# A DeltaNet and block-attention layer on one core: opening rebuilt, part of the low halves on GpSimd, order anew

## Chip, core and metric

The kernel runs on one core of one Trainium2 chip. The metric is device time in microseconds (us) of one execution; 236.81 us is the median of three runs of the kernel before (236.16 to 237.06). TensorE does the matrix work, VectorE and ScalarE elementwise work, GpSimd nearly nothing, and SyncE (SP) issues the DMAs.

## What is computed

One decoder layer for 256 tokens of width 1024, all in float32. `h` is a normalised `x`, scaled and shifted per column by two linear functions of a condition `c`. One wide product `h @ w_in` gives the inputs of two branches (gated DeltaNet with a short causal convolution; block attention, which for one block of 256 is causal attention) and the gates. Each branch is projected, the two are mixed, projected again, normalised, gated and added to `x`.

```python
shift, scale, gate = split(silu(c) @ w_ada + b_ada, 3)
h = rms_norm(x, g_pre) * (1 + scale) + shift
qkv_dn, z_dn, beta_logit, a_logit, qkv_mb, z_mb, merge_logit = split(h @ w_in, cuts)
qkv_dn = silu(causal_depthwise_conv(qkv_dn, conv_w))
o_dn = gated_delta_rule_chunked(l2_normalize(q_dn), l2_normalize(k_dn), v_dn, g, beta)
y_dn = (rms_norm(o_dn, dn_norm_g) * silu(z_dn)) @ w_proj_dn
y_mb = (moba_attention(q_mb, k_mb, v_mb) * silu(z_mb)) @ w_proj_mb
mixed = (sigmoid(m_dn) * y_dn + sigmoid(m_mb) * y_mb) @ w_out
out = x + gate * rms_norm(mixed, g_post)
```

## The kernel before

**Who sets the order.** `block_kernel` calls engine methods on a `Machine`, which records each one as an operation with its dependences (L107) and prices it (`price`, L125). `schedule` (L169) then lists all operations by rank, the longest priced way to the end, plus a number per stage from the table `BOOST` (L52); `issue` (L235) emits them. All instructions therefore have line 236 in the trace, and each engine runs its list strictly in order. `TURN` (L51) prices a change of TensorE between full-size matmuls, transposes and small-tile matmuls.

**Precision.** Weights and activations are split: `split` (L327) makes `whi`, a rounded copy, on ScalarE, and `wlo`, the rest (`raw` minus `whi`), on VectorE. Each product is three matmuls: hhi·whi, hlo·whi, hhi·wlo.

**Buffers and loads.** A weight chunk is 128 x 1024 (512 KB). There are 4 buffers `raw`, 5 `whi`, 5 `wlo`, 4 `wss`; all loads are issued by SP, one after the other in a fixed order, and a `raw` buffer is free for the next load only when its `wlo` has been made.

**Opening.** Loads: the small parameters `pr`, the two halves of `x` (128 tokens each), `wss` for k = 0, then `w1` and `wss` by turns (`load_k`, L353). TensorE runs warm-up matmuls and broadcasts silu(c) to all partitions (`scb`, L377, kept in buffer AT). Stage "x" (L388): ScalarE sums the squares of each half of `x`, VectorE makes 1/rms and a diagonal matrix `dg` (buffer pex), and 16 fp32 matmuls `xs @ dg` scale and transpose `x` into four PSUM banks. `ada(k)` (L419) makes shift and scale for 128 columns by two VectorE dot products of `wss` with AT. `h_ops(k)` (L431) makes hhi (ScalarE), a full copy (`cv`) and hlo (VectorE).

**First GEMM** (`phase1`, L438; stages "first", "cut", "mod", "ada"): eight steps k, each with two chunks of `w1`, 16 column blocks of 128, and three matmuls for each: 48 matmuls, into eight PSUM banks.

**After it:** `gemm_v` (L511, i = 6: value columns and the logits `lgw`), convolution, `gemm(i)` (L532, 15 jobs over `w2`, two chunks each, 48 matmuls each), norm (L601: transposes of q and k; ScalarE squares them for the norm, writing `jk`), attention scores (`mk`, `mq`, L642), the DeltaNet chunks, gates, projections, output. `gemm` matmuls are interleaved with all small work.

## Time and profile before

| | |
|---|---|
| median of 3 runs | 236.81 us (236.16 to 237.06) |
| the profiled execution's own time | 236.04 us |
| its span in the trace | 234.3 us |
| TensorE busy | 221.3 us, 1902 instructions |
| VectorE busy | 195.9 us, 442 |
| ScalarE busy | 142.4 us, 281 |
| GpSimd busy | 1.2 us, 7 |
| moved by DMA | 51.20 MB, mean 219 GB/s |

The page counts busy time per engine; the span is what the trace covers, and the execution's own time has 1.7 us more around it. Matmuls overlap in TensorE's pipeline and their ends are modelled, so a busy TensorE is judged by the distance of the starts. The idle time in square brackets stands ahead of an instruction, with what ended it.

### The profile page before, as it was taken

To read this page: it belongs to the slowest core of one execution; us is meant where nothing else is said; L and a number is where in the kernel's file an instruction comes from. 1 tells how busy PE (TensorE), PEld (TensorE's weight loads), DVE (VectorE), ACT (ScalarE), POOL (GpSimd) and SP (SyncE) were. 2 spreads that over 40 slices of the span, in tenths; PEclk is the share of its full clock that TensorE was granted. 3 is DMA by queue.
4 is the path that set the end of the run, shared out by engine and by line. 5 is a ranking of instruction groups with operands and counts; after the bars stand their busy time and mean duration, and the time that the engine had idled before them with its cause. 6 is when DMAs were issued, how large, how long until landed. Compare 5 with 4: busy or idle time off the path is not lost.

```text
span 234.3 us, 4925 instructions
## 1 busy us (share of the span) xinstructions
PE 221.3 (94%) x1902; PEld 209.0 (89%) x1902; DVE 195.9 (84%) x442; ACT 142.4 (61%) x281; POOL 1.2 (1%) x7
## 2 busy tenths in 40 slices
PE   8699999998999999999999999999999989999990
PEld 8699999997999998899789999888789979899980
DVE  0789998889899996499989999897899989668864
ACT  6585665556899589965416556445597943355341
POOL 1000000000000000000000000000000000000000
PEclk9799999999999999999999999999999999999999
DMA  7999999784879765252732507745396980297004
GB/s 220 377 413 406 411 404 388 280 304 158 314 238 312 233 220 183 91 179 65 267 120 92 180 21 236 228 131 174 94 369 246 261 289 26 70 325 236 0 29 153
DMA packets 15271, 51.20 MB, mean 219 GB/s; under 512 B 1680, under 2 KB 2064, under 8 KB 15248
## 3 DMA queue, kind: packets, MB, share of 16 engines
q1 hardware_dynamic: 15248, 50.89, 62.6%
q8 instruction: 15, 0.25, 0.4%
q14 instruction: 8, 0.07, 0.1%
HBM read 49.83 MB, written 1.05 MB: 217 GB/s over the span
## 4 chain that ended last, share of the span: by engine, by line
PE 50%; DMA 20%; DVE 14%; ACT 10%; issue 3%; SPq 1%; DVEq 0%; ACTq 0%
PE bank_g L236 32%; PE bank_d L236 14%; DMA raw<-in_w 10%; DMA wss<-in_wss 5%; PE bank_m L236 5%; DVE wlo L236 4%; ACT whi L236 3%; DVE wss L236 2%; ACT L236 2%; DMA raw<-in_wpj 2%; ACT jk L236 2%; DVE xT L236 2%; DMA raw<-in_wv 2%; DVE vT L236 1%; SPq L236 1%
## 5 line engine op out<-in xcount | busy, mean ns | idle before, releaser
L236 ACT CAST whi<-raw 128x1024 fp32r<-128x1024 f32 (+2 forms) x68 | 67.1, 993 | 38.3 <-DMA raw<-in_w 14.7
L236 DVE TENSOR_TENSOR wlo<-raw,whi 128x1024 fp32r<-128x1024 f32 (+2 forms) x68 | 77.8, 1158 | 8.0 <-ACT whi L236 6.7
L236 PE MATMUL bank_g<-hhi,whi 128*128 128x256 f32 x256 | 68.9, 282 | 0.9 <-DVE lgw L236 0.6
L236 PE MATMUL bank_g<-hhi,wlo 128*128 128x256 f32 x256 | 67.5, 277 | 0.0
L236 PE MATMUL bank_g<-hlo,whi 128*128 128x256 f32 x256 | 67.4, 277 | 0.0
L236 PEld LDWEIGHTS bank_g<-hhi,whi 128*128 128x128 f32 x256 | 47.5, 192 | 2.1 <-DVE lgw L236 0.8
L236 PEld LDWEIGHTS bank_g<-hhi,wlo 128*128 128x128 f32 x256 | 47.5, 192 | 0.4 <-issue 0.3
L236 PEld LDWEIGHTS bank_g<-hlo,whi 128*128 128x128 f32 x256 | 47.3, 192 | 0.4 <-issue 0.2
L236 PE MATMUL bank_g<-obh,whi 128*128 128x256 f32 x64 | 12.8, 281 | 1.0 <-DVE tl L236 1.0
L236 PE MATMUL bank_g<-obh,wlo 128*128 128x256 f32 x64 | 12.5, 275 | 0.0
L236 PE MATMUL bank_g<-obl,whi 128*128 128x256 f32 x64 | 12.4, 275 | 0.0
L236 DVE CUSTOM_DVE_ANT_0 wss<-wss,AT,pr 128x1024 f32<-128x1024 f32 x8 | 10.2, 1281 | 2.1 <-DMA wss<-in_wss 2.1
L236 PEld LDWEIGHTS bank_g<-obh,whi 128*128 128x128 f32 x64 | 9.9, 191 | 1.7 <-issue 1.3
L236 ACT ACT_TABLE_LOAD x8 | 10.3, 1283 | 1.6 <-DVE so L236 0.8
L236 DVE CUSTOM_DVE_ANT_0 wss<-wss,AT,b2g 128x1024 f32<-128x1024 f32 (+1 forms) x8 | 10.2, 1274 | 0.0
L236 PEld LDWEIGHTS bank_g<-obh,wlo 128*128 128x128 f32 x64 | 9.9, 192 | 0.2
L236 PE MATMUL bank_g<-whi,hhi 128*128 128x264 f32 (+1 forms) x32 | 8.9, 279 | 1.0 <-ACT whi L236 1.0
L236 PEld LDWEIGHTS bank_g<-obl,whi 128*128 128x128 f32 x64 | 9.7, 192 | 0.0
L236 PE MATMUL bank_m<-hhi,whi 128*128 128x256 f32 x48 | 9.2, 275 | 0.0
L236 ACT ACTIVATE pex<-sms,mx 128x256 f32<-128x256 f32 (+1 forms) x16 | 7.5, 480 | 2.6 <-DVE mx L236 2.5
L236 DVE SCALAR_TENSOR_TENSOR vT<-raw,sc,vT 128x1024 f32<-128x1024 f32 x7 | 8.9, 1275 | 0.0
L236 PE MATMUL bank_g<-wlo,hhi 128*128 128x264 f32 (+1 forms) x32 | 8.8, 276 | 0.0
(225 smaller groups left out, 445.4 us busy)
## 6 DMA issues: line engine op xcount, KB each, us to landing
raw<-in_w SPq DMA_DIRECT2D x43, 512.0 KB, 4.7
wss<-in_wss SPq DMA_DIRECT2D x15, 512.0 KB, 6.9
raw<-in_wg SPq DMA_DIRECT2D x8, 512.0 KB, 4.3
...
```

Source lines behind the costliest of these rows:

```text
L236: o["ins"] = getattr(self.engines[o["part"]], o["method"])(*o["args"], **o["kw"])
```

## The change

- **Opening.** The sum of squares of a half of `x` is split: columns 0 to 511 on ScalarE, 512 to 1023 on VectorE. `x` itself is scaled by 1/rms in place (three pieces of 128x512 on GpSimd, one on VectorE), then 16 transposes on TensorE replace the 16 fp32 matmuls. The shift for k = 0 is eight one-column matmuls; `wss[0]` is packed for that. The scale for k = 0 is a VectorE dot product in three pieces, and the two `wss` loads of k = 0 are cut into five. hhi for k = 0 moves to VectorE. The flag `strict` fixes the order on each engine in this part. Two warm-up matmuls are added.
- **GpSimd** makes `wlo` of the second chunk in steps 0 to 6 of the first GEMM and in seven `gemm` jobs (i even): 14 chunks.
- `lgw` is copied by ScalarE; the squares in norm write back into PSUM in place of `jk`.
- **Planner.** `TURN` becomes `turn(a, b)` with five kinds of small tiles, transposes count as full-size, some prices change, and the whole table `BOOST` is new, so the order changes throughout.

```diff
-WARM1, WARM2, ACTSQ = 5, 0, 0
+WARM1, WARM2 = 5, 2
...
-    TURN = 40.0, 120.0, 100.0
-    BOOST = dict(ada=33200, ada0=-46900, ...)
+    ENTER, BETWEEN, LEAVE = 95.0, 220.0, (0.0, 0.0, 330.0, 255.0, 230.0, 212.0)
+    BOOST = dict(ada1=-183500, ada3=27800, ...)
...
+        op["mode"] = self.kind(ins[0], out) if small and method != "transpose" else 0
+        if self.strict:
+            self.behind(op, [o for o in [self.latest.get(part)] if o])
+        self.latest[part] = op
...
+    def turn(self, a, b):
+        return 0.0 if a == b else self.ENTER if a == 0 else self.BETWEEN if b else self.LEAVE[a]
...
-    def split(t, name, cuts=1, width=D):
+    def split(t, name, cuts=1, width=D, by=None):
...
-            V.tensor_sub(lo[:, cs], t[:, cs], hi[:, cs])
+            (by or V).tensor_sub(lo[:, cs], t[:, cs], hi[:, cs])
...
+        if k == 0:
+            turns = [(0, lower), (1, lower), (0, upper), (1, slice(512, 768)), (1, slice(768, D))]
...
-        r = st[:, 2 + t : 3 + t]
-        V.tensor_scalar(r, st[:, t : t + 1], 1.0 / D, EPS, op0=mul, op1=add)
-        A.activation(r, r, AF.Sqrt)
-        V.reciprocal(r, r)
-        dg = mem([P, P], f"dg{t}", tag="pex")
-        V.tensor_scalar_mul(dg, ident, r)
-        for k in range(KT):
-            mm(xb[k // 2][...], xs[t][:, tok(k)], dg, t == 0 and k % 2 == 0)
...
+        A.activation(sq[:, lower], xs[t][:, lower], AF.Square, scale=D ** -0.5, accum_out=s0)
+        V.tensor_tensor_reduce(out=sq[:, upper], in0=xs[t][:, upper], in1=xs[t][:, upper], scale=1.0 / D, scalar=EPS, op0=mul, op1=add, accum_out=s1)
+        A.activation(r[t], s0, AF.Sqrt, bias=s1)
+        (A.copy if t else V.tensor_copy)(scb[:, 512 * t : 512 * t + 512], scb_bank[t])
+        V.reciprocal(r[t], r[t])
+        (V if t else G).tensor_scalar_mul(xs[t][:, lower], xs[t][:, lower], r[t])
+        G.tensor_scalar_mul(xs[t][:, upper], xs[t][:, upper], r[t])
+    sb = bank("g", "shift")
+    for q in range(KT):
+        mm(sb[:, 0:1], wss[0][:, tok(q)], sc[:, q : q + 1], q == 0, q == KT - 1)
...
+            T.transpose(xb[k // 2][...], xs[t][:, tok(k)], ident)
...
+            V.tensor_scalar(lies(hhi[0]), woven(xb[0][:, 0:S]), a, b, op0=mul, op1=add)
...
-        parts = [split(w1[k][i], f"w{k}{i}", cuts(k, i)) for i in range(2)]
+        parts = [split(w1[k][i], f"w{k}{i}", cuts(k, i), by=G if i and k < KT - 1 else V) for i in range(2)]
...
-            whi, wlo = split(raw("w2", 2 * i + j - 2 * (i > 6)), f"w2{i}{j}")
+            whi, wlo = split(raw("w2", 2 * i + j - 2 * (i > 6)), f"w2{i}{j}", by=G if j and i % 2 == 0 else V)
...
-                jk = mem([P, P], f"jk{n}{t}{h}", tag="jk")
-                A.activation(jk, pt[:, tok(h)], AF.Square, accum_out=...)
+                A.activation(pt[:, tok(h)], pt[:, tok(h)], AF.Square, accum_out=...)
```

TensorE in the opening, between the broadcast of silu(c) (`pr`, `sc`) and the first GEMM, before (`x_0` is x, `pex` the diagonal):

```order
L236 MATMUL bank_g_63<-pr_71,sc_83 128x128 x3
L236 MATMUL bank_g_64<-pr_71,sc_83 128x128 x3
L236 MATMUL bank_d_65<-pex_89,x_0_72 128x128 x2
L236 MATMUL bank_d_66<-pex_89,x_0_72 128x128
L236 MATMUL bank_d_67<-pex_89,x_0_72 128x128
```

and after (`pr` is here the identity, `ones` the warm-up, `sc,wss` the shift):

```order
L252 MATMUL bank_g_63<-pr_71,sc_83 128x128 x4
L252 MATMUL bank_g_64<-pr_71,sc_83 128x128 x4
L252 MATMUL bank_m_68<-ones_81 128x128 x2
L252 MATMUL bank_g_63<-sc_83,wss_73 128x1 x8
L252 MATMUL bank_d_65<-pr_71,x_0_72 128x128
L252 MATMUL bank_d_67<-pr_71,x_0_72 128x128
L252 MATMUL bank_m_69<-pr_71,x_0_72 128x128
```

The diagonal is gone, and the shift matmuls stand ahead of all transposes.

VectorE over the first steps of the first GEMM, before (`wss` rows are the dot products with their accumulator reads):

```order
L236 ISA wss_75,ab_110<-wss_75,AT_86,pr_71 128x1024
L236 ISA ab_110 128x1
L236 TENSOR_TENSOR hlo_0_102<-cv_112,hhi_0_94 128x256
L236 ISA wss_76,ab_110<-wss_76,AT_86,b2g_111,pr_71 128x1024
L236 ISA ab_110 128x1
L236 TENSOR_TENSOR wlo_124<-raw_78,whi_119 128x1024
L236 TENSOR_TENSOR wlo_125<-raw_79,whi_120 128x1024
L236 TENSOR_TENSOR hlo_0_103<-cv_113,hhi_0_95 128x256
```

and after:

```order
L252 TENSOR_TENSOR hlo_0_100<-cv_108,hhi_0_92 128x256
L252 ISA wss_75,ab_90<-wss_75,AT_86,pr_71 128x1024
L252 ISA ab_90 128x1
L252 ISA wss_76,ab_90<-wss_76,AT_86,b2g_91,pr_71 128x1024
L252 ISA ab_90 128x1
L252 TENSOR_TENSOR hlo_0_101<-cv_109,hhi_0_93 128x256
L252 ISA wss_73,ab_90<-wss_73,AT_86,pr_71 128x1024
L252 ISA ab_90 128x1
L252 ISA wss_74,ab_90<-wss_74,AT_86,b2g_91,pr_71 128x1024
L252 ISA ab_90 128x1
L252 TENSOR_TENSOR wlo_121<-raw_79,whi_116 128x1024
L252 TENSOR_TENSOR hlo_0_102<-cv_110,hhi_0_94 128x256
```

One `wlo` row per step is gone from VectorE. GpSimd's list from the same place on, after:

```order
L252 ISA
L252 TENSOR_SCALAR x_0_72<-x_0_72,st_84 128x512 x3
L252 TENSOR_TENSOR wlo_120<-raw_78,whi_115 128x1024
L252 TENSOR_TENSOR wlo_122<-raw_80,whi_117 128x1024
L252 TENSOR_TENSOR wlo_119<-raw_78,whi_114 128x1024
L252 TENSOR_TENSOR wlo_121<-raw_80,whi_116 128x1024
```

The first row without names is a GpSimd instruction of its own that the kernel before doesn't have; behind it stand the three pieces of `x`, then one `wlo` per step.

TensorE at the attention scores (`mk,mq`; the `xT` rows are small-tile matmuls of the DeltaNet part), before:

```order
L236 MATMUL bank_g_63<-hlo_0_103,whi_118 128x256
L236 MATMUL bank_g_63<-hhi_0_95,wlo_123 128x256
L236 MATMUL bank_m_70<-mk_131,mq_130 128x256
L236 MATMUL bank_d_67<-xT_87 128x256 x2
L236 MATMUL bank_m_68<-mk_131,mq_130 128x256
L236 MATMUL bank_d_65<-xT_87 128x256 x2
L236 MATMUL bank_g_63<-hhi_0_96,whi_118 128x256
```

and after:

```order
L252 MATMUL bank_g_63<-hhi_0_98,wlo_123 128x256
L252 MATMUL bank_m_70<-mk_127,mq_126 128x128
L252 MATMUL bank_m_68<-mk_127,mq_126 128x128
L252 MATMUL bank_m_70<-mk_127,mq_126 128x256
L252 MATMUL bank_m_68<-mk_127,mq_126 128x256
L252 MATMUL bank_m_69<-mk_127,mq_126 128x128
L252 MATMUL bank_g_63<-hhi_0_99,whi_118 128x256
```

The score matmuls now stand together, in two groups of which this is the first.

## Rows read from the trace of the kernel before

**Rows 1.** The page: busy time of each engine; the chain that ended last.

```profile
PE 221.3 (94%) x1902; PEld 209.0 (89%) x1902; DVE 195.9 (84%) x442; ACT 142.4 (61%) x281; POOL 1.2 (1%) x7
...
PE 50%; DMA 20%; DVE 14%; ACT 10%; issue 3%; SPq 1%; DVEq 0%; ACTq 0%
```

**Rows 2.** Windows by stage: start:end, length, busy (instructions) per engine, PEclk, DMA share, GB/s.

```profile
13.70:54.00 40.30, 40.10 (x352) 39.57 (x352) 37.46 (x56) 24.58 (x37) 0.00 (x0) 1.00 0.93 359
54.00:65.00 11.00, 9.44 (x82) 9.20 (x82) 9.50 (x19) 8.46 (x14) 0.00 (x0) 1.00 0.73 253
...
167.00:192.00 25.00, 23.71 (x200) 21.34 (x200) 22.94 (x43) 18.63 (x39) 0.00 (x0) 1.00 0.84 272
```

**Rows 3.** Timeline of all engines, 8 to 14 us: start, length, engine, work [idle before].

```profile
8.12 2.08 PE L236 MATMUL bank_d<-pex,x 128*128 128x128 f32 x8 [2.24 <-DVE pex L236]
8.37 1.28 DVE L236 CUSTOM_DVE_ANT_0 wss<-wss,AT,pr 128x1024 f32<-128x1024 f32 x1 [0.30 <-DMA wss<-in_wss]
...
10.22 1.28 ACT L236 CAST whi<-raw 128x512 fp32r<-128x512 f32 x2 [2.09 <-DMA raw<-in_w]
...
11.60 1.50 PE L236 MATMUL bank_d<-pex,x 128*128 128x128 f32 x12
...
13.73 0.49 PE L236 MATMUL bank_g<-hhi,whi 128*128 128x256 f32 x2 [0.18 <-ACT hhi L236]
```

**Rows 4.** Windows of the opening and of the first GEMM.

```profile
9.00:11.00 2.00, 2.00 (x11) 2.00 (x11) 2.00 (x5) 0.73 (x2) 0.00 (x0) 0.50 1.04 401
10.00:46.00 36.00, 35.65 (x307) 35.08 (x307) 33.04 (x48) 22.91 (x33) 0.00 (x0) 0.98 0.99 393
```

**Rows 5.** Timeline of ScalarE: casts of the first weight chunks of steps 1 and 2.

```profile
16.00 1.05 ACT L236 CAST whi<-raw 128x1024 fp32r<-128x1024 f32 x1
...
21.86 1.05 ACT L236 CAST whi<-raw 128x1024 fp32r<-128x1024 f32 x1 [2.88 <-DMA raw<-in_w]
```

**Rows 6.** VectorE's groups of 13.7 to 54 us: work, count, busy us, mean ns.

```profile
L236 DVE TENSOR_TENSOR wlo<-raw,whi 128x1024 fp32r<-128x1024 f32 x13 | 15.6, 1220 | 1.1 <-PE bank_m L236 0.7 <-ACT whi L236 0.4
L236 DVE CUSTOM_DVE_ANT_0 wss<-wss,AT,pr 128x1024 f32<-128x1024 f32 x7 | 9.0, 1280 | 1.8 <-DMA wss<-in_wss 1.8
L236 DVE CUSTOM_DVE_ANT_0 wss<-wss,AT,b2g 128x1024 f32<-128x1024 f32 x6 | 8.0, 1341 | 0.0
L236 DVE TENSOR_TENSOR hlo<-cv,hhi 128x256 fp32r<-128x256 f32 x8 | 3.4, 420 | 0.2 <-ACT cv L236 0.2
...
L236 DVE DVE_READ_ACCUMULATOR2_ANT ab<- 128x1 f32 x15 | 1.2, 81 | 0.0
```

**Rows 7.** TensorE's timeline: waits after 13.73 us.

```profile
28.65 0.38 PE L236 MATMUL bank_g<-hhi,whi 128*128 128x256 f32 x1 [0.17 <-ACT hhi L236]
...
55.05 0.38 PE L236 MATMUL bank_g<-whi,hhi 128*128 128x264 f32 x1 [1.01 <-ACT whi L236]
...
64.84 0.38 PE L236 MATMUL bank_g<-hhi,whi 128*128 128x256 f32 x1 [0.56 <-DVE lgw L236]
...
90.71 0.55 PE L236 MATMUL bank_d<-pr,xT 128*128 128x128 f32 x3 [0.17 <-ACT jk L236]
...
95.39 0.44 PE L236 MATMUL bank_d<-pr,vT 128*128 128x128 f32 x2 [0.22 <-ACT vT L236]
...
174.57 0.44 PE L236 MATMUL bank_m<-pr,pex 128*128 128x128 f32 x2 [0.30 <-ACT sms L236]
...
191.01 0.46 PE L236 MATMUL bank_g<-obh,whi 128*128 128x256 f32 x2 [0.99 <-DVE tl L236]
```

**Rows 8.** TensorE's timeline around one group of small-tile matmuls.

```profile
141.32 0.28 PE L236 MATMUL bank_g<-hhi,wlo 128*128 128x256 f32 x1
141.44 0.28 PE L236 MATMUL bank_g<-hhi,whi 128*128 128x256 f32 x1
141.64 1.12 PE L236 MATMUL bank_d<-vT,bt 64*64 64x32 f32 x32
142.69 0.38 PE L236 MATMUL bank_g<-hlo,whi 128*128 128x256 f32 x1
```

**Rows 9.** GpSimd's timeline: its one cast.

```profile
1.00 0.29 POOL L236 CAST onesr<-ones 128x128 fp32r<-128x128 f32 x1
```

More of the change, by code (lines that the diff above doesn't have):

```diff
@@ L116, in record, with kind @@
         return op
+    @staticmethod
+    def kind(l, out):
+        k, m = list(l.ap)[0][1], list(out.ap)[0][1]
+        return 3 if k > 64 else 2 if m > 64 else 5 if k <= 32 else 4
+    def turn(self, a, b):
+        return 0.0 if a == b else self.ENTER if a == 0 else self.BETWEEN if b else self.LEAVE[a]
     @staticmethod
@@ L165, in wait @@
         if o["part"] == u["part"] and o["method"] != "dma_start":
-            return 0.0 if kind == "anti" or o["part"] == "PE" else o["late"]
+            return 0.0 if kind == "anti" or o["part"] == "PE" else 130.0 if o["part"] == "ACT" else o["late"]
         return self.HOP + (o["late"] if kind == "data" or o["part"] == "PE" or o["method"] == "dma_start" else 0.0)
@@ L220, in schedule @@
                     window += 1
-                held = held * slow + (self.TURN[o["mode"]] if mode != o["mode"] else 0.0)
+                held = held * slow + self.turn(mode, o["mode"])
                 mode = o["mode"]
@@ L345, in block_kernel @@
     wss, w1 = {}, {}
+    lower, upper = slice(0, 512), slice(512, D)
     def pieces_of(n):
-        return (slice(0, 512), slice(512, D)) if n == 2 * KT - 1 else (slice(0, D),)
+        return (lower, upper) if n == 2 * KT - 1 else (slice(0, D),)
     def cuts(k, i):
@@ L355, in load_k @@
             wss[n] = mem([P, D], f"wss{n}", tag="wss")
-            for c in pieces_of(n):
-                load(wss[n][:, c], I["wss"][n][:, c])
+        if k == 0:
+            turns = [(0, lower), (1, lower), (0, upper), (1, slice(512, 768)), (1, slice(768, D))]
+        else:
+            turns = [(n, c) for n in (2 * k, 2 * k + 1) for c in pieces_of(n)]
+        for n, c in turns:
+            load(wss[n][:, c], I["wss"][n][:, c])
         w1[k] = [raw("w1", 2 * k + i, cuts(k, i)) for i in range(2)]
@@ L374, in block_kernel @@
         mm(warm[:, 0:P], ones, ones, True)
+    M.stage("scb")
+    M.strict = True
     scb = mem([P, D], "scb", tag="AT")
@@ L382, in block_kernel @@
             last = mm(b[:, tok(j)], sc[:, r : r + 1].to_broadcast([P, P]), ident, j == 0)
-        (A.copy if i else V.tensor_copy)(scb[:, i * 512 : i * 512 + 512], b)
+        scb_bank = [b] if i == 0 else scb_bank + [b]
     for n in range(WARM2):
-        M.behind(mm(warm[:, 0:P], ones, ones, True), [last])
+        mm(warm[:, 0:P], ones, ones, True)
     M.stage("x")
@@ L390, in block_kernel @@
     xb = [bank(tag, f"xb{q}") for q, tag in enumerate(("d", "d", "d", "m"))]
+    r = [st[:, 3 * t + 2 : 3 * t + 3] for t in range(NT)]
     for t in range(NT):
         sq = mem([P, D], f"sq{t}", tag=("mv", "DT")[t])
-        if t >= ACTSQ:
-            A.activation(sq, xs[t], AF.Square, accum_out=st[:, t : t + 1])
-        else:
-            V.tensor_tensor_reduce(out=sq, in0=xs[t], in1=xs[t], scale=1.0, scalar=0.0, op0=mul, op1=add, accum_out=st[:, t : t + 1])
-        r = st[:, 2 + t : 3 + t]
@@ L398, in block_kernel @@
[L398 to L407 removed]
+        s0, s1 = st[:, 3 * t : 3 * t + 1], st[:, 3 * t + 1 : 3 * t + 2]
@@ new lines, in block_kernel @@
+    M.strict = False
+    V.tensor_scalar_add(b2g, pr[:, PSI_B2 : PSI_B2 + 8], 1.0)
+    V.tensor_mul(b2g, b2g, pr[:, PSI_GP : PSI_GP + 8])
+    M.strict = True
+    for n, c in enumerate((lower, slice(512, 768), slice(768, D))):
+        to = ab[:, 0, 1:2]
+        V.tensor_tensor_reduce(
+            out=wss[1][:, c], in0=wss[1][:, c], in1=scb[:, c], scale=pr[:, PSI_GP : PSI_GP + 1], scalar=to if n else b2g[:, 0:1],
+            op0=mul, op1=add, accum_out=to,
+        )
+    M.strict = False
@@ L408, in block_kernel @@
+    for k in range(4, KT):
+        for t in range(NT):
+            M.stage("x", f"t{k}")
+            T.transpose(xb[k // 2][:, (k % 2) * S + t * P : (k % 2) * S + (t + 1) * P], xs[t][:, tok(k)], ident)
+    M.stage("x")
     acc1 = [bank(tag, f"acc{n}") for n, tag in enumerate(("g", "g", "m", "m", "d", "d", "d", "m"))]
@@ L432, in h_ops @@
         hf = mem([P, S], f"hf{k}", tag="cv")
-        for h in (hhi[k], hf):
-            A.activation(lies(h), lies(xT[:, k]) if k else woven(xb[0][:, 0:S]), AF.Identity, bias=ab[:, k, 0:1], scale=ab[:, k, 1:2])
+        a, b = ab[:, k, 1:2], ab[:, k, 0:1]
+        if k:
+            A.activation(hhi[k], xT[:, k], AF.Identity, bias=b, scale=a)
+            A.activation(hf, xT[:, k], AF.Identity, bias=b, scale=a)
+        else:
+            V.tensor_scalar(lies(hhi[0]), woven(xb[0][:, 0:S]), a, b, op0=mul, op1=add)
+            A.activation(lies(hf), woven(xb[0][:, 0:S]), AF.Identity, bias=b, scale=a)
+            A.copy(lies(xT[:, 1]), woven(xb[0][:, S : 2 * S]))
+            for q in range(1, 4):
+                A.copy(lies(xT[:, 2 * q : 2 * q + 2].rearrange("p k s -> p (k s)")), woven(xb[q]))
         V.tensor_sub(hlo[k], hf, hhi[k])
@@ L450, in block_kernel @@
         M.stage("ada", k)
-        ada(k)
+        if k:
+            ada(k)
         M.stage("mod", k)
@@ L653, in scores @@
                 op = mm(s_[:, 0:128] if q.start == 0 else s_[:, 128:384], mqT[pp, pair, q], mkT[pp, pair, k], q.start == 0)
-                op["cost"] = 110.0 if q.start == 0 else 215.0
+                op["cost"] = 107.0 if q.start == 0 else 213.0
                 M.behind(op, turns[-1:])
```

38 lines of the change are left out of this document (19 added, 19 removed).

## The prediction

> **What bounds the kernel now.** I read the page first. TensorE is busy for 94% of the span and half of the chain that ended last is TensorE; DMA has 20% of the chain, VectorE 14% [rows 1]. So nearly everything that can be won is TensorE idle time or work taken from TensorE, and the matmul count hardly changes. The second view is the table by stage: in the first GEMM (13.7 to 54 us) TensorE is busy for 40.10 of 40.30 us and VectorE for 37.46; in 54 to 65 us TensorE loses 1.56; in 167 to 192 us it loses 1.29 [rows 2]. The third is the timeline: the first GEMM matmul starts at 13.73 us, and what is ahead of it is a chain of small steps [rows 3]. The fourth is TensorE's timeline with the waits [rows 7]. A matmul starts 0.11 to 0.12 us after the one ahead and is drawn 0.28 long [rows 8], so a drawn wait of 1.01 costs 1.01 + 0.17 = 1.2 us, and so on. The reader should see that after 13.73 us there are nine such waits and that they cost 5.2 us together: 0.3 at 28.65, 1.2 at 55.05, 0.7 at 64.84, 1.4 in four waits from 90.71 to 95.39 (the first and the last stand in the rows), 0.5 at 174.57 and 1.2 at 191.01.
>
> One step k of the first GEMM has three limits that are nearly equal. TensorE: 48 matmuls at 40.30/352 = 0.1145 us make 5.5. VectorE: two dot products with wss (1.28 and 1.34), two reads of the accumulator (0.08 each), two low parts (1.22 each) and hlo (0.42) make 5.64 [rows 6]. DMA: four loads of 512 KB are 2.10 MB, at the 393 GB/s of 10 to 46 us, where the DMA engines are busy for 0.99 of the time, 5.3 [rows 4]. Taking one of the three down gains little there by itself.
>
> **The opening, part by part.** Removed are 16 fp32 matmuls against a diagonal; 16 transposes take their place. Twelve of the old ones took 1.50 us at the later clock, 0.125 each, and the first eight took 2.08, 0.26 each [rows 3], in a stretch where the granted clock was 0.50 of 2.4 GHz, the 1.2 GHz level [rows 4], after TensorE had been idle (2.24 of idle stand ahead of the matmuls at 8.12). Also removed from VectorE is the dot product that made the shift of k = 0, 1.28 us at 8.37; eight one-column matmuls make it. Three things must now come together ahead of the first GEMM matmul. (a) The first half of the weights: its cast starts on landing at 10.22 and two halves take 1.28 [rows 3], so 10.9. (b) The scale dot product in three pieces: the chunk that it reads must have landed by the time the same dot product starts in the kernel before, right behind the row at 8.37, so by about 9.6; its last quarter takes some 0.4 and hhi for k = 0 another 0.6, so 10.8. (c) The transposes: they stand behind the shift matmuls, which need wss[0] whole: its dot product started at 8.37 on landing [rows 3], and a quarter megabyte of wss[1] now lands ahead of its second half, 0.26 MB at 393 GB/s or 0.7 us, so about 8.9; 16 of them at 0.125 are 2.0, at 0.26 4.2, and I take the slow ones for the first half, since TensorE pauses here as before: 9.1 + 3.0 = 12.1. So the first GEMM matmul comes at about 12, 1.6 to 1.7 us sooner.
>
> What is late next is the data. The first weight chunk of step 2 landed at 21.86, and its cast takes 1.05 [rows 5], so 23.1 with the hand-over. TensorE, 2 x 5.5 us ahead of it, gains nothing from a start before 12.1. The two limits meet, and I take 13.73 - 12.2 = **1.5 us gained**. Better end: 2.7 (start at 11.0, loads sooner too, since raw buffers come free sooner). Worse end: 0. Three of the four halves of x are now scaled on GpSimd, whose only row of this kind is a cast of 128 columns in 0.29 us [rows 9]; 512 columns are 0.29 to 1.16, at 1.16 they end at 6.0 + 3 x 1.16 = 9.5, in time for the last transposes. At twice that they end at 13, and the gain is gone. The scaling is an instruction form on GpSimd that the trace of before doesn't have, with a further instruction ahead of it that I can't price either; by its place it has over 4 us of cover, from about 1.3 to about 6 us.
>
> **GpSimd's low parts.** Seven of the sixteen chunks in the first GEMM and seven in the second go from VectorE to GpSimd. VectorE goes from 5.64 to 4.42 us per step. By itself that saves nothing where TensorE was already busy for 40.10 of 40.30; it can save the waits that VectorE or a raw buffer caused. The load of the gemm_v weights was issued late, behind buffers that come free only after a low part, and TensorE waited 1.2 for their cast at 55.05; lgw on VectorE, waited for at 64.84, goes to ScalarE; the wait at 28.65 came from hhi. Of these 2.2 us I take **1.6 gained**, bounds 0.4 to 2.2. The cost: a GpSimd subtraction of 128x1024 isn't in the trace. Below, it is no faster than VectorE's 1.22; above, by the cast, 8 x 0.29 = 2.33 with one input and 4.7 if two inputs double it. Each is under a step of 5.5, and they come one per step, later one per two GEMM jobs, so GpSimd keeps pace even at the upper end. What a slow one does is to deliver late and to hold its raw buffer, and with it all loads that stand behind on SP, which issues in order: 2.33 - 1.22 = 1.1 and 3.5 at most, once, where TensorE, which runs in order, stands at the matmul with wlo. The planner places that matmul last of its three. I take **0.6 lost**, bounds 0 and 3.5, nearer to the lower, since the pace is kept.
>
> The Trainium skill, GPSIMD Engine Reference, section "Elementwise — side-by-side cycle accounting", has 4497 ns for a two-input add of 2048 columns; half of that is an estimate of 2.2 us. No run here shows it; the sum would stay as it is.
>
> **Order and turns.** Small-tile groups on TensorE that are entered from full-size matmuls go from 16 to 12. Entering costs 0.09: from 141.44 to 141.64 is 0.20 where 0.11 is usual; leaving about 0.10: the next full-size matmul starts 0.07 before the drawn end of the group where 0.17 is usual [rows 8]. Four pairs are 0.8; one more turn between two small kinds gives some back: **0.5 gained**, bounds 1.0 gained and 0.5 lost. The squares that follow the norm's transposes lose their separate output buffer, and the transposes stand in 16 groups in place of 9. That is aimed at the four waits between 90.7 and 95.4; ScalarE has the same squares to do, so I take **0.8** of 1.4, bounds 0 and 1.4. The two late waits hang on VectorE's and ScalarE's order at 174.57 and 191.01 [rows 7]: another order removes them or makes others; **0.9** of 1.7, bounds 0 and 1.7. Three more DMA issues on SP stand in the opening, all with earlier loads still landing ahead of them: 0. The last rows of ScalarE, VectorE and SP stand in the same order as before: 0.
>
> **Sum.** -1.5 - 1.6 + 0.6 - 0.5 - 0.8 - 0.9 = -4.7 against the profiled execution's own 236.04 us: 231.3. That execution was 0.77 below the median of the runs, so in terms of the median **232.1 us**. All the good ends together give -9.1 + 0.77, so about 228; without GpSimd's cost at its upper end, the bad ends give about the time of before.
>
> **Rivals.** *First, VectorE and GpSimd exclude each other (slower).* The trace of before has GpSimd busy for 1.2 us in all [rows 1], none of it beside a VectorE row of the first GEMM, so it can't tell. If a GpSimd subtraction can't run while VectorE reads two SBUF operands, then a step costs VectorE and GpSimd 4.42 + 2.33 = 6.75 in a row, against 5.5 on TensorE. It decides from the point where a GpSimd subtraction takes more than 5.5 - 4.42 = 1.1 us, so at its lower bound already. Seven steps at 1.25 are 8.8 us; gemm_v's matmuls and the sooner start fill some, so the end of gemm_v moves from 64.8 to 67 or 70. Less 2.2 for the later gains, plus 1 to 2 for the second GEMM, where VectorE has little to spare, the time is about 240 (236.5 to 243). For it: nearly all of VectorE's work in a step reads two operands [rows 6]. Against it: ScalarE, VectorE and TensorE read SBUF side by side in every step, and VectorE's low parts keep to 1.22 us whatever runs beside them. A chance of 0.20.
>
> The Trainium skill states just this rule: SBUF — State Buffer, section "Who interferes with whom", says that a VectorE instruction with two SBUF inputs contends with a GpSimd instruction that reads SBUF, and that whoever comes first holds the shared ports for its whole instruction. No run here shows it yet.
>
> *Second, the waits only move.* TensorE's idle time after 13.73 is 5.2 us because the order was fitted to the old durations; a new order with GpSimd late in some places has its own waits, and the opening's gain is eaten by the data of steps 1 to 3: 0 to -2, so 234.5 to 237.5. For it: three limits within 5% in the first GEMM. A chance of 0.20, a third of it with a gain that still shows.
>
> *Third, everything goes right,* 228 to 229: a chance of 0.05.
>
> **Chances.** The forecast (229 to 234.5) has 0.55. A measurement of this kernel tells about 0.5%, 1.2 us, from no change: faster is below 235.6, slower above 238. Faster: 0.55 + 0.05 + 0.06 = 0.66. Slower: 0.18 of the first rival and 0.01 of the second, 0.19. The same: 0.15. The range from 228.8 to 239.5 leaves out half of the first rival's chance and most of the third's. The forecast's own range is 229 to 234.5.
>
> **What would show it.** Right: first GEMM matmul near 12; step 2's first low matmuls near 23; no wait near 55 and 65; VectorE near 4.4 us per step; GpSimd's rows of 128x1024 between 1.2 and 2.4 with VectorE's at their old 1.22. Wrong: VectorE's two-input rows longer than 1.22 or idle ahead of them whenever GpSimd runs (first rival); TensorE waiting for wlo or whi in 13.7 to 54; the x halves scaled only after 10 us; waits of the old size at new places after 90 us.

## The result, and the profile after

The changed kernel takes 251.75 us (median of 4 executions, 251.23 to 259.63) against 236.92 us for the kernel before on the same chip: 1.0626 times as long, with a 95% interval of 1.0588 to 1.0664. It is **slower by 15 us** where 232.1 was predicted, and beyond the range. Here and below, ratios leave out executions that took over 1.5% longer than the fastest of the same kernel on that chip; medians in us are over all executions.

The page after, busy times and the chain (compare [rows 1]):

```profile
PE 224.5 (90%) x1906; PEld 212.3 (85%) x1906; DVE 200.6 (80%) x430; ACT 141.7 (57%) x283; POOL 43.7 (18%) x24
...
PE 47%; DVE 21%; DMA 15%; issue 7%; ACT 7%; SPq 2%; DVEq 0%; ACTq 0%
```

TensorE has nearly the same work (224.5 us, 221.3 before) in a span 15 us longer. VectorE, which gave away 14 low parts of 1.22 us, is busy for longer than before, 200.6 us against 195.9, and it has moved up in the chain from 14% to 21%. What TensorE waits for is the first clue; the view lists TensorE's waits by releaser (us in total, times, longest):

```profile
PE bank_g L252 <- DVE wlo L252: 4.5, 4, 1.4
PE bank_d L252 <- DVE vT L252: 3.9, 1, 3.9
PE bank_g L252 <- ACT lgw L252: 2.6, 1, 2.6
PE bank_d L252 <- POOL wlo L252: 1.7, 3, 0.9
PE bank_d L252 <- DVE sm L252: 1.5, 1, 1.5
```

GpSimd's own low parts are waited for 1.7 us in all; VectorE's rows for 4.5, 3.9 and 1.5. VectorE's groups from the first GEMM on (compare [rows 6]; columns: work, count, busy us, mean ns) show why:

```profile
L252 DVE CUSTOM_DVE_ANT_0 wss<-wss,AT,b2g 128x1024 f32<-128x1024 f32 x6 | 11.6, 1940 | 0.8 <-DMA wss<-in_wss 0.8
L252 DVE CUSTOM_DVE_ANT_0 wss<-wss,AT,pr 128x1024 f32<-128x1024 f32 x7 | 10.3, 1475 | 2.4 <-DMA wss<-in_wss 2.4
L252 DVE TENSOR_TENSOR wlo<-raw,whi 128x1024 fp32r<-128x1024 f32 x6 | 9.5, 1581 | 0.0
L252 DVE TENSOR_TENSOR hlo<-cv,hhi 128x256 fp32r<-128x256 f32 x8 | 6.5, 808 | 1.4 <-ACT cv L252 1.2
```

The same four kinds took 1.34, 1.28, 1.22 and 0.42 us before; they now average 1.94, 1.48, 1.58 and 0.81. Row by row, GpSimd's and VectorE's timelines (start, length, engine, work; POOL is GpSimd, DVE is VectorE):

```profile
27.10 3.20 POOL L252 TENSOR_TENSOR wlo<-raw,whi 128x1024 fp32r<-128x1024 f32 x1 [5.51 <-ACT whi L252]
31.16 2.48 POOL L252 TENSOR_TENSOR wlo<-raw,whi 128x1024 fp32r<-128x1024 f32 x1 [0.86 <-ACT whi L252]
```

```profile
27.98 3.41 DVE L252 TENSOR_TENSOR wlo<-raw,whi 128x1024 fp32r<-128x1024 f32 x1
31.31 2.62 DVE L252 TENSOR_TENSOR hlo<-cv,hhi 128x256 fp32r<-128x256 f32 x1
```

The low part at 27.98 is held until GpSimd's row ends at 30.30 and then takes its 1.1 us; hlo at 31.31, 0.42 us of work, lasts until GpSimd's next row ends at 33.64, and a little longer. The other way round, GpSimd's row of 3.20 us started while VectorE worked on a dot product, and took 0.8 us more than its usual 2.39. Later in the kernel the victims are tiny:

```profile
110.85 2.38 POOL L252 TENSOR_TENSOR wlo<-raw,whi 128x1024 fp32r<-128x1024 f32 x1 [18.55 <-ACT whi L252]
...
128.30 4.40 POOL L252 TENSOR_TENSOR wlo<-raw,whi 128x1024 fp32r<-128x1024 f32 x1 [15.08 <-ACT whi L252]
...
141.67 2.40 POOL L252 TENSOR_TENSOR wlo<-raw,whi 128x1024 fp32r<-128x1024 f32 x1 [5.54 <-ACT whi L252]
...
152.28 2.56 POOL L252 TENSOR_TENSOR wlo<-raw,whi 128x1024 fp32r<-128x1024 f32 x1 [8.21 <-ACT whi L252]
```

```profile
111.02 2.24 DVE L252 COPY sm<-ss 128x8 f32<-128x8 f32 x1
```

```profile
128.09 2.36 DVE L252 TENSOR_TENSOR wlo<-raw,whi 128x1024 fp32r<-128x1024 f32 x2
```

```profile
141.80 2.38 DVE L252 TENSOR_TENSOR X<-X,tm 128x96 f32<-128x96 f32 x1
...
152.65 2.23 DVE L252 TENSOR_TENSOR X<-X,tm 128x16 f32<-128x16 f32 x1
...
157.83 0.87 PE L252 MATMUL bank_d<-vT,bt 64*64 64x32 f32 x20 [3.92 <-DVE vT L252]
```

A copy of 8 columns (0.17 alone) takes 2.24 us, two additions of 96 and 16 columns (0.25 and 0.17 alone) take 2.38 and 2.23, and TensorE, whose DeltaNet chain hangs on them, waits 3.92 us at 157.83. At 128 us VectorE came first and ran two low parts back to back; there GpSimd's row took 4.40. Twelve VectorE rows beside GpSimd are longer than their kind alone, by 19.8 us together; 14 x 1.22 = 17.1 us had been taken off VectorE.

Not everything is stretched. The convolution, which reads one operand from PSUM and one from SBUF, ran beside GpSimd at its usual pace, three rows in 1.26 us:

```profile
68.29 2.38 POOL L252 TENSOR_TENSOR wlo<-raw,whi 128x1024 fp32r<-128x1024 f32 x1 [13.05 <-ACT whi L252]
```

```profile
68.33 1.26 DVE L252 SCALAR_TENSOR_TENSOR cv<-bank_d,pr,cv 128x255 f32<-128x255 f32 x3
```

### The profile page after: what moved, and what is told of

The parts are those of the page before. It is cut to its first block, busy times and chain, and to the rows that moved or that the text cites. A ratio compares the mean times of both kernels' runs of the same rounds, so it can differ in the third digit from the quotient of the medians.

```text
span 249.3 us, 4978 instructions
## 1 busy us (share of the span) xinstructions
PE 224.5 (90%) x1906; PEld 212.3 (85%) x1906; DVE 200.6 (80%) x430; ACT 141.7 (57%) x283; POOL 43.7 (18%) x24
## 3 DMA queue, kind: packets, MB, share of 16 engines
HBM read 49.83 MB, written 1.05 MB: 204 GB/s over the span
## 4 chain that ended last, share of the span: by engine, by line
PE 47%; DVE 21%; DMA 15%; issue 7%; ACT 7%; SPq 2%; DVEq 0%; ACTq 0%
PE bank_g L252 30%; DMA wss<-in_wss 12%; PE bank_d L252 11%; PE bank_m L252 5%; DVE wlo L252 5%; DMA raw<-in_wo 3%; DVE X L252 3%; DVE vT L252 2%; DVE wss L252 2%; ACT bank_d L252 2%; DVE xT L252 2%; SPq L252 2%; ACT whi L252 1%; DVE cv L252 1%; DVE sm L252 1%
## 5 line engine op out<-in xcount | busy, mean ns | idle before, releaser
L252 PE MATMUL bank_g<-hhi,wlo 128*128 128x256 f32 x256 | 69.2, 285 | 4.5 <-DVE wlo L252 4.5
L252 DVE TENSOR_TENSOR wlo<-raw,whi 128x1024 fp32r<-128x1024 f32 (+3 forms) x54 | 64.1, 1200 | 9.7 <-ACT whi L252 9.7
L252 PE MATMUL bank_g<-hlo,whi 128*128 128x256 f32 x256 | 69.6, 286 | 0.7 <-DVE hlo L252 0.7
L252 POOL TENSOR_TENSOR wlo<-raw,whi 128x1024 fp32r<-128x1024 f32 x14 | 37.3, 2665 | 102.8 <-ACT whi L252 102.8
L252 PEld LDWEIGHTS bank_g<-hhi,whi 128*128 128x128 f32 x256 | 48.9, 198 | 3.8 <-ACT lgw L252 2.8
L252 PEld LDWEIGHTS bank_g<-hlo,whi 128*128 128x128 f32 x256 | 48.7, 197 | 2.1 <-DVE hlo L252 1.1
L252 DVE CUSTOM_DVE_ANT_0 wss<-wss,AT,b2g 128x1024 f32<-128x1024 f32 (+1 forms) x8 | 15.6, 1949 | 2.4 <-DMA wss<-in_wss 2.4
L252 ACT ACTIVATE hhi<-xT,ab 128x256 fp32r<-128x256 f32 x7 | 4.2, 601 | 19.4 <-DVE ab L252 19.4
L252 DVE SCALAR_TENSOR_TENSOR cv<-bank_d,pr,cv 128x255 f32<-128x255 f32 (+2 forms) x18 | 7.9, 476 | 3.1 <-ACT cv L252 3.0
L252 PE MATMUL bank_d<-hhi,wlo 128*128 128x256 f32 x48 | 7.6, 281 | 1.7 <-POOL wlo L252 1.7
```

The source lines that it names most:

```text
L252: o["ins"] = getattr(self.engines[o["part"]], o["method"])(*o["args"], **o["kw"])
```

## The experiments

In all of them the kernel before was timed on the same chip, and its median was between 235.6 and 236.6 us. "Order kept" means that the planner's list is issued as it was, and only the engine of the named operations is changed when they are issued. Where an opening of one kernel is put ahead of the rest of the other, the list is put together from both.

### What the low parts on GpSimd cost: taken back, and done alone

```diff
 def issue(self):
     for o in self.schedule():
-        o["ins"] = getattr(self.engines[o["part"]], o["method"])(*o["args"], **o["kw"])
+        part = "DVE" if (o["part"], o["method"]) == ("POOL", "tensor_sub") else o["part"]
+        o["ins"] = getattr(self.engines[part], o["method"])(*o["args"], **o["kw"])
```

> The changed kernel with its order kept, but the 14 low parts that GpSimd made are issued on VectorE at the same place of the order. Theory (GpSimd's reading shuts out VectorE instructions that read two SBUF operands for GpSimd's whole 2.4 us): VectorE gets 14 x 1.22 = 17.1 us of work and loses about 19 us of stretched rows, so its busy total stays near 200 us, but no wss, hlo or X row is longer than alone; the time falls to 236 to 242 us. Rival A (the new order and the new opening make the waits): it stays at 248 to 252. Rival B (only GpSimd's slowness, 2.4 against 1.22, delivers late): TensorE's waits for GpSimd's wlo were 1.7 us, so it falls to about 250.

Measured: 242.0 us, 1.0257 (1.019 to 1.0325). VectorE's groups are back at their lengths, and the two waits of TensorE that mark the way are:

```profile
L253 DVE TENSOR_TENSOR wlo<-raw,whi 128x1024 fp32r<-128x1024 f32 x13 | 15.9, 1220 | 0.7 <-ACT whi L253 0.7
L253 DVE CUSTOM_DVE_ANT_0 wss<-wss,AT,pr 128x1024 f32<-128x1024 f32 x7 | 9.0, 1284 | 3.9 <-DMA wss<-in_wss 3.8
L253 DVE CUSTOM_DVE_ANT_0 wss<-wss,AT,b2g 128x1024 f32<-128x1024 f32 x6 | 8.0, 1339 | 0.0
...
L253 DVE TENSOR_TENSOR hlo<-cv,hhi 128x256 fp32r<-128x256 f32 x8 | 3.4, 423 | 1.4 <-ACT cv L253 1.2
```

```profile
69.49 0.38 PE L253 MATMUL bank_g<-hhi,whi 128*128 128x256 f32 x1 [1.90 <-ACT lgw L253]
```

```profile
147.91 0.77 PE L253 MATMUL bank_d<-vT,bt 64*64 64x32 f32 x20 [0.51 <-DVE vT L253]
```

The order is the same in both kernels, so places can be compared: the first matmul after gemm_v stands at 69.49 here and at 72.91 in the changed kernel (3.4 us), the DeltaNet group at 147.91 and at 157.83 (9.9), the end at 238.3 and 249.3 (11.0 in the two profiled executions; 9.8 in the medians). So a third of the loss is made by the end of gemm_v, and most of the rest between there and the DeltaNet group, where the three short rows of VectorE's serial chains are stretched: 1.0 us more at TensorE's wait for sm (1.49 in the changed kernel, 0.49 here), 3.4 more at its wait for vT.

The reverse, the kernel before with its order kept and the same 14 low parts issued on GpSimd:

```diff
-            V.tensor_sub(lo[:, cs], t[:, cs], hi[:, cs])
+            V.tensor_sub(lo[:, cs], t[:, cs], hi[:, cs])["to"] = to   # "POOL" for the 14
...
-            o["ins"] = getattr(self.engines[o["part"]], o["method"])(*o["args"], **o["kw"])
+            o["ins"] = getattr(self.engines[o.get("to", o["part"])], o["method"])(*o["args"], **o["kw"])
```

> The kernel before with its order kept, but the same 14 low parts issued on GpSimd: the move alone, without a new plan. Theory (exclusion): some 8 to 14 VectorE rows stretched by up to 2.4 us, 15 to 20 us in all, and the time rises by 6 to 12 us, to 242 to 248. Rival (it was the new plan that made things slow in the run that planned anew with these low parts): within 2 us of the kernel before.

Measured: 1.0373 (1.0299 to 1.0448), which is 245.1 against 236.1 us: 9 us. That rests on two executions, 245.01 and 245.18 us; the other two took 252.15 and 253.46, and the profiled one is the first of these. Its granted clock is 1.00 up to 152 us and 0.50 from 156 to 170, so its trace is read up to 154 only: eleven VectorE rows are stretched, by 19.1 us together. One pair:

```profile
26.18 2.91 POOL L236 TENSOR_TENSOR wlo<-raw,whi 128x1024 fp32r<-128x1024 f32 x1 [3.23 <-ACT whi L236]
```

```profile
26.75 3.43 DVE L236 CUSTOM_DVE_ANT_0 wss<-wss,AT,b2g 128x1024 f32<-128x1024 f32 x1
```

The split is another one here: the first matmul after gemm_v stands at 71.22 against 64.84 in the kernel before, 6.4 us later already, and a DeltaNet group at 153.88 against 144.67, 9.2 us.

Both ways give 9 to 10 us for the move alone. Late delivery (rival B, about 250) and the rival of the second run (within 2 us) are out. Rival A, order and opening, explains none of these 9 to 10 us; the other 6 us, which the first run left standing, are its part.

### A new plan is not a small edit

Two runs made the same edits through the planner, with the stage tables as they were: the changed kernel with `by=V` everywhere, and the kernel before with `by=G` for the 14.

> The changed kernel with all low parts on VectorE and the order planned anew for that (same table). Theory: no exclusion, the opening's gain of 1.5 us stays: 233 to 238 us. Rival A (order and opening): 246 or more.

> The kernel before with only this part of the change: the same 14 low parts on GpSimd, planned by its own planner. Theory: wss, hlo and X rows that meet GpSimd's stretch by up to 2.4 us, and the time rises by 8 to 16 us, to 245 to 253. Rival A: within 2 us of the kernel before. Rival B: 2 to 3 us slower.

Measured: 265.14 us (1.1242) and 266.1 us (1.1299), far above both forecasts; the first lies where its rival A stood. It has no low part on GpSimd, and VectorE's rows are of normal length from the first GEMM on; it loses its time in an order that doesn't fit:

```profile
180.00:212.00 32.00, 17.61 (x104) 14.87 (x104) 28.37 (x40) 13.31 (x31) 0.00 (x0) 0.72 0.67 230
```

```profile
210.12 0.79 PE L252 MATMUL bank_g<-obh,whi 128*128 128x256 f32 x2 [3.72 <-ACT obh L252]
```

In 180 to 212 us TensorE is busy for 17.61 of 32, VectorE for 28.37. The same 14 operations move as in the first experiment, which took 242.0 with the order kept: 23 us of difference from letting the planner plan anew. So the times of these two runs say nothing on GpSimd, and all further runs keep an order, but for the one with writes below, whose time isn't used.

### Which kind of access shuts VectorE out

In the first run GpSimd copies `raw` into `wlo` (one input), order kept. In the second GpSimd only writes: 56 times a scratch buffer of 128x512 is set to zero, the 14 low parts are left out (`whi` stands in for them), and the order is planned anew. The edit of the first:

```diff
+            if (o["part"], o["method"]) == ("POOL", "tensor_sub"):
+                o["ins"] = self.engines["POOL"].tensor_copy(o["args"][0], o["args"][1])
```

> The changed kernel with its order kept, but GpSimd copies raw into wlo in place of subtracting (one input; the result is wrong by that). If any reading of SBUF by GpSimd shuts out VectorE: stretched wss, hlo and X rows as in the changed kernel, shortened with GpSimd's row; time 245 to 252. If only a second input on GpSimd's side does it: all VectorE rows at 1.22, 1.28, 1.34, 0.42, time below 246.

> The changed kernel without the 14 low parts of GpSimd (whi is used twice in their place, so the result is wrong by the low part); GpSimd instead sets a scratch buffer of 128x512 to zero 56 times, writing without reading. If writing shuts VectorE out too, wss and wlo rows beside it are longer than 1.22 to 1.34 us. If only reading does, they keep their lengths although GpSimd is busy beside them for 10 us and more. The order is planned anew, so the whole time tells nothing.

With one input GpSimd's row is 1.04 us, and VectorE rows that meet it are still stretched, by no more than that row: 3.1 us in five rows. The first of the pair is GpSimd's, the second VectorE's (0.25 alone):

```profile
133.92 1.08 POOL L253 CAST wlo<-raw 128x1024 fp32r<-128x1024 f32 x1 [5.41 <-PE bank_g L255]
```

```profile
134.16 0.94 DVE L255 TENSOR_TENSOR X<-X,tm 128x96 f32<-128x96 f32 x1
```

The time was 239.04 us, below the 245 expected; it is one execution and has no interval. It fits that the shutting out is as long as GpSimd's row. With writing alone, GpSimd's 51 rows and VectorE's run side by side, all at their own lengths:

```profile
L252 POOL MEMSET scratch<- 128x512 f32 x51 | 26.8, 525 | 2.9
```

```profile
L252 DVE CUSTOM_DVE_ANT_0 wss<-wss,AT,b2g 128x1024 f32<-128x1024 f32 x6 | 8.1, 1343 | 0.8 <-DMA wss<-in_wss 0.7
L252 DVE CUSTOM_DVE_ANT_0 wss<-wss,AT,pr 128x1024 f32<-128x1024 f32 x6 | 7.7, 1283 | 5.5 <-DMA wss<-in_wss 5.5
L252 DVE TENSOR_TENSOR wlo<-raw,whi 128x1024 fp32r<-128x1024 f32 x5 | 6.1, 1220 | 0.0
```

So it is GpSimd's reading that does it. Last, the other side: the kernel before, order kept, with only the three low parts that meet the convolution.

> The kernel before, its order kept, with only three low parts on GpSimd: those of the second chunks of the first three jobs with even number, which in the changed kernel ran beside VectorE rows that read one operand from PSUM (the convolution) and stretched nothing. Theory (only VectorE instructions with two SBUF operands are shut out): at most 1.5 us of stretched rows, and the time stays within 0.4% of the kernel before. Rival (any work beside GpSimd is slowed): 5 us or more of stretched rows and 1% slower.

Measured: 0.9984 (0.9958 to 1.001), one row stretched, by 0.5 us. Three GpSimd rows of 2.4 us cost nothing there, and they gain nothing either: TensorE's only wait from 60 to 95 us is the one for lgw, 0.72 (0.56 in the kernel before).

### The opening

Three edits: x scaled on VectorE instead of GpSimd (order of the changed kernel kept); the new opening ahead of the whole rest of the kernel before, with the order of each part as it was in its own kernel; the same with step 0 in the new order too.

> The changed kernel with its order kept, but the three pieces of x that GpSimd scaled (1.7 us each) are scaled on VectorE (0.5 each). Theory: GpSimd's share of the opening costs little: the first GEMM matmul moves from 12.15 to between 11.3 and 12.5 and the whole time changes by less than 1.5 us from 251.75. Rival A: the opening is the cause, and the time falls by more than 4 us.

> The changed kernel's opening (x scaled on GpSimd and VectorE, then transposed; shift on TensorE; scale in three pieces) ahead of the rest of the kernel before: no low parts on GpSimd, lgw and jk as before, and the order of all later work kept as in the kernel before. Theory (the opening is worth what the sum says, the slowing is the low parts on GpSimd and the new order): the first GEMM matmul near 12.1 to 12.4 us and 1 to 2 us less than the kernel before, 234 to 235. Rival A (the opening's gain is eaten by the data of steps 1 and 2): within 0.7 us of before. If it is slower by more than 1 us, the opening itself costs.

> The new opening and the new order of step 0 of the first GEMM, and from step 1 on the order of the kernel before; no low parts on GpSimd, lgw and jk as before. In the earlier try with the old order of step 0 TensorE waited 1.5 us for the second chunk's cast, which stands behind four xT copies in the new opening. Theory (that wait was the mismatch of the two orders): it falls below 0.3 us and the time to between 0.5% below and 0.3% above the kernel before. Rival (the opening costs by itself): 0.6 to 0.9% slower, as in the earlier try.

Measured: 252.4 us with x on VectorE (1.0664, 1.0592 to 1.0737; the changed kernel had 1.0626), so GpSimd's scaling isn't the matter, though in the changed kernel the first two pieces of the scale, beside it, took 1.06 and 0.90 us, and 0.81 and 0.54 here. The first GEMM matmul came at 13.63 in that profile and not earlier, at a granted clock of 0.50 from 10 to 16 us. The opening alone is 1.0076 (1.0048 to 1.0105), and 1.0078 (1.005 to 1.0105) with step 0 in the new order, which took the wait of 1.5 us for the cast away: **the new opening costs 1.8 us** where 1.5 gained was forecast, and the mismatch of orders isn't the cause. The windows of the last run show what may be (start:end, length, busy of PE, PEld, DVE, ACT, POOL, then the granted clock, DMA share, GB/s), with the first GEMM matmul below:

```profile
8.00:10.00 2.00, 1.48 (x8) 1.50 (x9) 0.77 (x3) 0.00 (x0) 1.55 (x2) 0.68 1.07 395
10.00:12.00 2.00, 2.00 (x11) 2.00 (x12) 1.93 (x8) 0.09 (x1) 1.78 (x1) 0.50 1.05 418
12.00:14.00 2.00, 2.00 (x11) 2.00 (x10) 0.29 (x3) 1.20 (x3) 0.07 (x1) 0.50 1.02 408
```

```profile
8.53 3.35 PE L331 MATMUL bank_g<-sc,wss 128*128 128x1 f32 x16 [1.87 <-DMA wss<-in_wss]
...
15.04 0.56 PE L331 MATMUL bank_g<-hhi,whi 128*128 128x256 f32 x1
```

TensorE waits 1.87 us for wss ahead of the shift, which now stands ahead of everything; its granted clock is 0.50 (1.2 GHz) from 10 to 14 us, the shift takes 3.35 us where its two halves took 1.02 and 1.05 in the changed kernel's profile, and the transposes start 0.21 apart instead of 0.11. The first GEMM matmul comes at 15.04, against 13.73 in the kernel before. In the changed kernel's profile the shift began 1.4 us sooner, at 7.16, and the clock stayed at 1.00; the start was at 12.15. Of the ten profiles here with the new opening and no further warm-up matmuls it is the only one without the low clock; the other nine start between 12.28 and 15.43. So the pause was filled, with 4 and 12 further warm-up matmuls in the new opening, and with 8 and 18 in the kernel before:

```diff
+            if o["n"] == self.filler[0]:
+                for _ in range(self.filler[1]):
+                    self.engines["PE"].matmul(*self.filler[2], start=True, stop=True, skip_group_check=True)
```

> The same with 4 further warm-up matmuls ahead of the shift, which fill about 0.9 us of TensorE's pause. Theory: the granted clock of 8 to 16 us is more often 1.00, and the time is 0.2 to 0.6% below the run without them, so 0.2 to 0.8% below the kernel before. Rival (the clock of the opening is worth nothing since the data of steps 1 and 2 come no sooner): equal to the run without them.

> The new opening ahead of the old order (0.8% slower than before), with 12 further warm-up matmuls between the broadcast of silu(c) and the shift, so that TensorE's pause of 1 to 2 us ahead of the shift is filled. Theory (the new opening loses its gain since TensorE pauses twice in it and then works its transposes and first GEMM matmuls at a granted clock of 0.50): the clock stays at 1.00 from 8 to 16 us, the first GEMM matmul comes at 11.8 to 12.6, and the time falls by 1.5 to 3 us, to within 0.5% of the kernel before or below it. Rival (the loss is the arrival of wss and of the weights, whatever the clock): it stays 0.6 to 0.9% above the kernel before.

> The kernel before, its order kept, with 8 further warm-up matmuls in TensorE's pause from 5.9 to 8.1 us (18 of them ended at 10.1 and kept the first diagonal matmuls waiting for 2 us, and the kernel was still 0.5% faster). Theory: 8 end at about 7.8, the clock stays at 1.00, the first GEMM matmul comes at 13.2 to 13.5, and the kernel is 0.3 to 0.8% faster than before. Rival (the 0.5% came from elsewhere): within 0.2% of before.

> The kernel before, its order kept, with 18 further warm-up matmuls in TensorE's pause from 5.9 to 8.1 us. Theory: the clock of 8 to 11.5 us goes from 0.50 to 1.00 and the first 16 diagonal matmuls take 2 us in place of 3.4, but the second half of x waits for VectorE until 11.2 anyway, so the first GEMM matmul moves from 13.73 to 13.2 to 13.6 and the time by less than 0.5 us, within 0.3% of before. Rival (the half clock in the opening is what bounds it): 1.2 us or more faster.

Measured: 1.0031 (1.0007 to 1.0056) with 4, 1.0024 (0.9981 to 1.0066) with 12 and the old order of step 0; 0.9978 (0.995 to 1.0007) and **0.9952 (0.9924 to 0.9979)** in the kernel before with 8 and 18; the last is the only interval that lies below 1. It is a small effect: over all twelve executions the medians with 18 and before are 235.58 and 236.13 us, 0.9977, and with 12 in the new opening 238.04, 1.0081, as much as without them. In time 8 and 18 missed their forecasts (0.3 to 0.8% faster, and within 0.3%); 4 met the one against the run without them and missed the one against the kernel before.

With the pause filled the clock of 8 to 14 us is 1.00 in all four profiles, but the start is what was hoped for in one. In the new opening the first GEMM matmul comes at 12.39 with 4 and at 13.20 with 12 (11.8 to 12.6 expected). In the kernel before it comes at 13.97 with 8 and at 14.02 with 18 (13.6 at the latest expected), no sooner than its 13.73:

```profile
14.02 0.49 PE L236 MATMUL bank_g<-hhi,whi 128*128 128x256 f32 x2
```

So in the old opening the clock doesn't set the start, and what gave the 0.5% there stays open. In the new one the 4 matmuls take back 1.1 of the 1.8 us (1.0031 against 1.0078, on the same chip), so the low clock is part of what it costs. The rest can only be argued from the trace: the gain at the start does not last. TensorE's first GEMM matmul of the new opening with 4 more, the cast and hhi of step 3 on ScalarE, and TensorE's wait for gemm_v:

```profile
12.39 0.57 PE L331 MATMUL bank_g<-hhi,whi 128*128 128x256 f32 x3
```

```profile
27.61 1.04 ACT L331 CAST whi<-raw 128x1024 fp32r<-128x1024 f32 x1 [1.93 <-DMA raw<-in_w]
28.57 0.60 ACT L331 ACTIVATE hhi<-xT,ab 128x256 fp32r<-128x256 f32 x1
```

```profile
55.68 0.38 PE L331 MATMUL bank_g<-whi,hhi 128*128 128x264 f32 x1 [1.07 <-ACT whi L331]
```

1.34 us are gained at the start (12.39 against 13.73). Ahead of 29.22 TensorE loses 1.3 us, since the weights of step 3 land at 27.6 and their cast and hhi follow on ScalarE; at 55.68 it waits 1.07 for the gemm_v weights, and that is 0.6 later than the same matmul of the kernel before, at 55.05 [rows 7]. That the data is the next limit was a sentence of the prediction; that it takes back everything was part of its second rival.

### The new order by itself

> The kernel before's opening and step 0 of the first GEMM, and from step 1 on the order of the changed kernel, with lgw on ScalarE and the squares in place as in the change, but all low parts on VectorE. It prices the new order (with these two small edits) by itself. Theory (the three causes add up): the changed kernel with its low parts on VectorE was 2.6% slower, the opening alone 0.8%, so the order costs the rest: 1.2 to 2.2% slower than the kernel before, with TensorE waiting 1.5 to 3 us after gemm_v for the copies behind ScalarE's table load. Rival (the order costs nothing by itself, and only goes badly with the new opening): within 0.5%.

> The changed kernel with its order kept, the 14 low parts on VectorE as in the first experiment (242.0 us), and the lgw copy, which the change moved to ScalarE, back on VectorE. Theory: lgw stood on ScalarE behind a cast that waits for a buffer and behind a table load; TensorE's wait of 2.1 us there shrinks below 0.8 and the time falls by 1 to 2 us, to 240 to 241. Rival (the wait has another releaser, mv or xT on ScalarE): it stays at 242.

> The first experiment's kernel (order of the changed kernel, 14 low parts on VectorE, 2.6% slower than before) with one more edit: the copies mv and lgw that empty the two banks of gemm_v stand on ScalarE ahead of the activation that needs a table load, and not behind it. Theory (TensorE's wait of 2.1 to 2.7 us after gemm_v is the table load of 1.28 and what stands with it): the wait falls below 1.2 us and the time by 1 to 3 us, to 1.3 to 2.2% above the kernel before. Rival (the wait hangs on VectorE or on the banks themselves): it stays at 2.6%.

The old opening and the new order from step 1 on, low parts on VectorE: 1.0148 (1.0116 to 1.0181), 3.5 us slower. So the causes add up: 3.7% (low parts) + 1.5% (order) + 0.8% (opening) = 6.0%, and 6.3% were measured. The order's share is taken with lgw and the squares as in the change. Its largest single wait after the opening is the one after gemm_v; ScalarE's list ahead of it, and the wait:

```profile
66.06 1.28 ACT L315 ACT_TABLE_LOAD   x1
67.35 0.42 ACT L315 ACTIVATE xT<-cv 128x256 f32<-128x256 f32 x1
67.68 0.35 ACT L315 COPY mv<-bank_g 128x256 f32<-128x256 f32 x1
67.93 0.17 ACT L315 COPY lgw<-bank_g 128x8 f32<-128x8 f32 x1
```

```profile
68.15 0.38 PE L315 MATMUL bank_g<-hhi,whi 128*128 128x256 f32 x1 [1.96 <-ACT lgw L315]
```

The copies mv and lgw, which free gemm_v's bank for the next job, stand behind a table load and an activation, and TensorE waits 1.96 us. In the kernel before ScalarE's table load ran where it was waiting for weights anyway, and TensorE waited 0.56 at 64.84 [rows 7]:

```profile
59.46 1.28 ACT L236 ACT_TABLE_LOAD   x1
...
61.64 1.05 ACT L236 CAST whi<-raw 128x1024 fp32r<-128x1024 f32 x1 [0.47 <-DMA raw<-in_w]
```

Two edits of the first experiment's kernel were meant to take the wait away: lgw back on VectorE gave 1.0291 (1.0212 to 1.037), the copies ahead of the table load 1.0246 (1.021 to 1.0283), neither told from its 1.0257. In the first lgw stands behind a low part and two rows of the convolution on VectorE, and the wait is 2.50. In the second the table load is behind, but a cast that itself waits for TensorE is ahead of the copies, and the wait is 1.86. Neither edit took the wait away, so neither tests what it is worth; that the table load's place is the cause stays argued, not shown.

## Why the prediction was wrong

**The step that failed** is the 0.6 us lost to GpSimd's low parts. GpSimd kept pace, as forecast. The price of one came out right by chance (2.33 taken, 2.39 measured): 2.33 stood for one input, which took 1.04 in the copying run, and two inputs were put at up to 4.7. What was wrong is the sentence that it then only delivers late: the move measured 9 to 10 us, because each of its rows keeps VectorE from reading two SBUF operands for as long as it lasts, while GpSimd's own lateness is 1.7 us of TensorE's waits. This was the first rival, with 0.20. What was set against it, that the other engines read SBUF side by side, was no evidence on GpSimd, which had no row beside them. The Trainium skill, SBUF — State Buffer, section "Who interferes with whom", states the rule, down to an instruction that only writes being harmless; the traces here agree on each point that they touch (hlo 0.42 to 2.62, memset rows beside 1.22 us low parts). A specific rule that the trace can't contradict deserved more than a fifth.

**The rival was also priced too low,** at 240. It counted throughput in the first GEMM (5.5 against 6.75 us a step), and by the end of gemm_v that made 3.4 us in one comparison and 6.4 in the other, where 2 to 5 stood. It did not count latency: rows of 0.17 to 0.25 us on a serial chain that become 2.2 to 2.4, three of them for 6.3 us. And it had the order's gains of 2.2 in it, which were losses.

**The opening:** start at 12.1 forecast, 12.15 in the changed kernel's profile, and that is luck. The path was another: all transposes ran at the full clock, the last of them waited until 11.38 for GpSimd's x (its pieces took 1.74 us on average, where up to 1.16 had been taken), and the first GEMM matmul followed hhi on VectorE, which ended at 12.00 and had been put at 10.8. And it is the earliest of ten profiles. The 0.125 and 0.26 us for a transpose were misread too: the old rows hold two records for each fp32 matmul, 32 for the 16, and a transpose has one, 0.11 after the one ahead at full clock. The term of 1.5 us gained is 1.8 lost, and 0.7 lost with the pause filled. The halved clock of the transposes was in the working, as the slow half of them; but the forecast took it as the kernel before had it, and not that TensorE waits once more, for wss ahead of the shift, and that the clock is then low in nine of ten profiles. The rest, as argued above, is the data of step 3: the working named that of step 2, and let it meet the gain instead of exceeding it.

**The waits:** those at 28.65, 55.05 and 64.84, 1.6 gained in the sum. In the changed kernel the one at 55 has given way to one of 0.95 at 57.84, for a low part on VectorE, and the one after gemm_v is 2.58 instead of 0.56. lgw's move to ScalarE was counted as a gain; nothing was asked about what stands ahead of it on ScalarE's list. **The norm:** 0.8 forecast, nothing: three waits of 0.3, 0.4 and 0.7 where four made 1.4. **The late waits:** 0.9 forecast; one of 0.54 at 194.09 remains where 1.29 were drawn, so this size came out right. **Turns:** no run separates them; in sum the new order lost 3.5 us where 2.2 (turns, norm and late waits together) had been counted as gained.

**Sum.** Low parts, opening and order were forecast at 1.0, 1.5 and 2.2 us gained (1.6 less 0.6 for the first) and measured at 9, 1.8 and 3.5 lost. Two sums of the working are 0.1 off and move nothing: the nine waits make 5.3, the good ends 9.0.
